# The last feed-forward stage of a hybrid trunk: the activations' sums moved ahead on VectorE, a weight sum by DMA, two subtractions moved

## The chip, the cores and the metric

The kernel runs on one core of a Trainium2 chip, in one launch. The metric is the device time in microseconds, the median of several executions. Below, PE is TensorE, DVE is VectorE, ACT is ScalarE, POOL is GpSimd and SP is SyncE; a name with a small q (SPq, POOLq, ACTq) is the queue of that engine, where it issues DMAs and waits on semaphores.

## The reference

A trunk of two layers on x (1, 512, 1024) in float32, each layer a token mixer and a SwiGLU feed-forward block (FFN), each with a norm before and behind it, and with shift, scale and gate from a conditioning vector. The part around the change is the last FFN:

```python
D_FF = 2816
def swiglu_ffn(h, w_in, w_out):
    gate, up = jnp.split(h @ w_in, 2, axis=-1)
    return (jax.nn.silu(gate) * up) @ w_out

h = rmsnorm(x, norm_g[i, 2]) * (1.0 + scale) + shift
y = swiglu_ffn(h, f_w_in[i], f_w_out[i])
x = x + gate * rmsnorm(y, norm_g[i, 3])
```

## The kernel before, in words

Every matrix product is taken with operands split into a high and a low part (`fp32r`): high x high, high x low and low x high, so three matmuls for one. A split is a cast on ACT (the high part) and a subtraction on DVE (the low part). Weights are loaded by DMAs from SP's queue into staging buffers (`wst`, two of them), split into `whl` (four buffers), and used by PE.

In the last FFN the order of the instructions on every engine is the order of the lines in the code. Both products of this stage are done with seven multiplications of half-size blocks instead of eight, as in Strassen's method, so sums and differences of activations and of weights are formed first.

*The lead and the whole chunks.* The hidden size 2816 is 22 column tiles of 128 for gate and 22 for up. Before the stage, six accumulations (`lead_ps[0..5]`, in the trace `li`) are begun for gate 0, gate 1, up 0, up 1, gate 2 and gate 3; `rest(i)` issues the second half of one of them. Two whole chunks follow (`more`, in the trace `ip`), for up 2 and up 3. `gate(f, pst)` (ACT) takes the silu, `up(f, pst)` (DVE, L1603) multiplies and writes `raw[:, f]`.

*The activations' sums.* `value(j)` (L1804) adds the high and low part of `h[j]` back together, into `va` (for j < 4, in a staging buffer of tag `wst`) or `vb`. `t_one` to `t_four` form differences of the token halves and split them into `tq`, the moving operands of P5, P6, P7 and P4. `t_low` is one split: the cast (L1807) and the subtraction (L1809, L1811).

*The unit loop.* Sixteen units u of 256 columns (two tiles) follow, alternately gate and up. `fetch(u)` issues the loads of a unit on SP's queue (L1626, L1627 into `sg`; L1629, L1630, L1632 into a staging buffer, `wsu`) and two accumulating DMAs on POOL's queue. `fetch(u + 2)` is issued as unit u begins. Each unit is seven products of 12 matmuls: P1, (P7 of the unit before), P5, P2, (P4 of the unit before), P6, P3. `split_x`, `split_y`, `split_z` and `split_s` make their weights, from sums by `sum_y` (L1666) and `sum_s` (L1670). `keep` copies a bank out on ACT (L1697), `c11`, `c12`, `c22` (L1713) and `c21` finish the four quarters of the output, and c21 of an up unit multiplies by the gate (L1721).

*The sums for the second product.* `s13` (L1593, L1594) forms two differences of quarters of `raw`, as soon as four tiles of `raw` are complete. `raw_done` calls it, from `up` or from c21.

*The second product.* Its weights lie in nine units (two of two row pairs, seven of one; a row pair p is 256 rows), in quarters `b11`, `b12`, `b21`, `b22`, loaded by `w2_load`. 77 steps, seven for each of 11 row pairs, are done two to a tile: 39 tiles n, each of 12 matmuls of 512 columns. Seven groups of steps follow one another: A (b11, a11), B (b21, a12), C (b22, a12), A (b22, a11), D (b12, s1), A (b11, a21), A (b21, a22); the trace calls their banks cA, cB, cC, cD. `w_prep(n + 4)` and `a_prep(n + 3)` prepare later tiles behind the matmuls of tile n (ACT L1743 and L1756, DVE L1744 and L1757). In between the weight quarters are changed in place: t1 (b12 += b11), t2 (b22 += b12) and t4 (b21 += b22) by accumulating DMAs on POOL's queue (L1619, SBUF to SBUF), t3 (b11 = b22 - b11) by a tensor operation on POOL (L1790). `behind(n)` says after which tile each is issued; t3 of row pair p stands behind tile 14 + p, t4 of unit i behind tile 14 + i.

Of the kernel before, what the change touches and what calls it, by code (L numbers as in the profile page):

```python
# [17 lines left out]
T = 512  # L18
# [17 lines left out]
def trunk_kernel(  # L36
# [533 lines left out]
    with ExitStack() as ph:  # L570
# [398 lines left out]
        def gate(f, pst):  # L969
            gates[f] = t2("g")  # L970
            act.activation(gates[f], pst, AF.Silu)

        def up(f, pst):
            g, a = gates[f], act_tile(f"ff{f}")
            dve.tensor_mul(g, pst, g)
            act.copy(a[:, 0, :], g)
            acts.append(a)
            lows.append(lambda: dve.tensor_tensor(a[:, 1, :], g, a[:, 0, :].bitcast(F32), SUB))
# [563 lines left out]
    with ExitStack() as ph:  # L1542
# [4 lines left out]
        NP = NF // 2  # L1547
# [28 lines left out]
        def b_(i, name, q=None):  # L1576

            t = rows_of[i][int(name[1]) - 1][:, :, slice(0, T) if name[2] == "1" else slice(T, D)]
            return t if q is None else t[:, q, :]

        def a_(name, p, n=1):
            if name == "s1":
                return s1t[:, p:p + n, :]
            c = int(name[2]) - 1
            v = raw[:, 2 * p:2 * (p + n), :].rearrange("p (i c) t -> p i c t", c=2)
            return v[:, :, c, slice(0, 256) if name[1] == "1" else slice(256, T)]
# [2 lines left out]
            gates[f] = t2("g")  # L1589
            act.activation(gates[f], pst, AF.Silu)  # L1590

        def s13(p, n):
            dve.tensor_tensor(a_("s1", p, n), a_("a21", p, n), a_("a22", p, n), SUB)  # L1593
            dve.tensor_tensor(a_("a21", p, n), a_("a11", p, n), a_("a21", p, n), SUB)  # L1594

        def raw_done(f):
            if f % 4 == 3:
                s13(f // 2 - 1, 2)
            elif f == NF - 1:
                s13(f // 2, 1)  # L1600

        def up(f, pst):
            dve.tensor_mul(raw[:, f, :], pst, gates[f])  # L1603
# [177 lines left out]
        with tc.manual_schedule(engines={PE_ENGINE, mybir.EngineType.SP, mybir.EngineType.Activation,  # L1781
# [2 lines left out]
            def t1(i):  # L1784
                add_(b_(i, "b12"), b_(i, "b11"))

            def t3(p):
                i = unit_of[p]
                q = units[i].index(p)
                pool.tensor_tensor(b_(i, "b11", q), b_(i, "b22", q), b_(i, "b11", q), SUB)  # L1790

            def t2_(i):
                add_(b_(i, "b22"), b_(i, "b12"))
# [9 lines left out]
                dst = va[:, j, :] if j < 4 else vb[j // 2 - 2][:, j % 2, :]  # L1803
                dve.tensor_add(dst, h[j][:, 0, :].bitcast(F32), h[j][:, 1, :].bitcast(F32))  # L1804

            def t_low(dst, src, sign=1.0):
                act.activation(dst[0], src, AF.Copy, scale=sign)  # L1807
                if sign == 1.0:
                    dve.tensor_tensor(dst[1], src, dst[0].bitcast(F32), SUB)  # L1809
                else:  # L1810
                    dve.scalar_tensor_tensor(dst[1], src, sign, dst[0].bitcast(F32), MUL, SUB)  # L1811

            def tq_of(i, ks):
                return [tq[i // 2][:, i % 2, hl, ks, :] for hl in range(2)]

            def t_one():
                dve.tensor_tensor(va[:, :, LO], va[:, :, LO], va[:, :, HI], SUB)
                t_low(tq_of(0, slice(0, 4)), va[:, :, LO])

            def t_two(b):  # L1820
                k = slice(2 * b, 2 * b + 2)
                dve.tensor_tensor(va[:, k, HI], vb[b][:, :, HI], va[:, k, HI], SUB)
                dve.tensor_add(vb[b][:, :, HI], vb[b][:, :, HI], va[:, k, LO])
                t_low(tq_of(1, k), vb[b][:, :, HI], -1.0)

            def t_three():
                t_low(tq_of(2, slice(0, 4)), va[:, :, HI])

            def t_four(b):
                k = slice(2 * b, 2 * b + 2)  # L1830
                dve.tensor_tensor(vb[b][:, :, LO], vb[b][:, :, HI], vb[b][:, :, LO], SUB)
                t_low(tq_of(3, k), vb[b][:, :, LO])

            for i, f in ((0, 0), (2, 0), (1, 1), (3, 1), (4, 2), (5, 3)):
                rest(i)
                if i in (2, 3):
                    up(f, lead_ps[i])
                else:
                    gate(f, lead_ps[i])
                if i == 1:  # L1840
                    for j in range(4):
                        value(j)
                elif i == 3:
                    t_one()
                elif i == 4:
                    for j in range(4, 8):
                        value(j)
            acc = in_chunk(more[0], h)
            split_x(0)
            for b in range(2):  # L1850
                t_two(b)
            sum_y(0)
            split_y(0)
            t_three()
            fetch(1)
            acc2 = in_chunk(more[1], h)
            sum_s(0)
            up(2, acc)
            split_s(0)
            for u in range(UN):  # L1860
                v = u - 1
                last = u == UN - 1
                if u + 2 <= UN:
                    fetch(u + 2)
                elif last:
                    tail = []
                    n12 = load_w([(w1, 21 * P, P), (w1, DFF + 20 * P, P)], later=tail)
                product(u, "P1")
                if u:
                    c12(v)  # L1870
                else:
                    up(3, acc2)
                    for b in range(2):
                        t_four(b)
                split_x(u + 1)
                if u:
                    product(v, "P7")
                keep(u, "A", 0, LO)
                product(u, "P5")
                if u:  # L1880
                    c22(v)
                product(u, "P2")
                keep(u, "C", 1, HI)
                if u:
                    product(v, "P4")
                c11(u)
                split_z(u)
                if not last:
                    sum_y(u + 1)
                    sum_s(u + 1)  # L1890
                product(u, "P6")
                if u:
                    c21(v)
                if last:
                    for op in tail[0]:
                        op()
                    n3 = load_w([(w1, DFF + 21 * P, P)], later=tail)
                else:
                    split_y(u + 1)
                product(u, "P3")  # L1900
                keep(u, "A", 0, HI)
                if not last:
                    split_s(u + 1)
# [24 lines left out]
            a_prep(0)  # L1928
            w_prep(0)
            tiles.append(in_chunk(n3[0], h))  # L1930
            up(20, tiles[2])
            w2_tile(4)
            w2_load(4, "b11")
# [1 line left out]
            a_prep(1)  # L1935
            w_prep(1)
            up(21, tiles[3])

            ht = [hp.tile([P, 1, D], F32, tag=f"h{j}", name=f"w2h{j}") for j in range(KD)]
            for i in range(5, len(units)):  # L1940
# [42 lines left out]
            def behind(n):  # L1983

                for i, u in enumerate(units):
                    if n - 8 == u[-1] // 2:
                        t2_(i)
                if 14 <= n < 14 + NP:
                    t3(n - 14)
                    if n - 14 < len(units):  # L1990
                        t4(n - 14)
                for t in range(2):
                    if n == 5:
                        got["11", t] = t2("c11")
                        act.copy(got["11", t], bank["A"][t])
                    elif n == 10:
                        dve.tensor_add(got["11", t], got["11", t], bank["B"][t])
                    elif n == 16:
                        got["12", t] = t2("c12")
                        act.copy(got["12", t], bank["C"][t])  # L2000
                    elif n == 21:
                        dve.tensor_tensor(got["12", t], got["12", t], bank["A"][t], SUB)
                    elif n == 27:
                        dve.tensor_add(got["12", t], got["12", t], bank["D"][t])
                        got["22", t] = spare[f"c22_{t}"]
                        act.copy(got["22", t], bank["D"][t])
                    elif n in (29, 30):
                        if t == n - 29:
                            square(t, 0, got["11", t])
                            square(t, 1, got["12", t])  # L2010
                    elif n == 32:
                        dve.tensor_tensor(got["22", t], got["22", t], bank["A"][t], SUB)  # L2012
                    elif n == 34:
                        square(2 + t, 0, got["22", t])
                        mean(t)
                        mean(2 + t)
                    elif n == 35:
                        root(t)
                        gated(got["22", t], 1, got["22", t])
                if n == 35:  # L2020
                    for t in range(2):
                        for hf, c in enumerate(("11", "12")):
                            x_new(t, hf, gated(got[c, t], hf, got[c, t]))
# [54 lines left out]
```

## Time and profile before

| | us |
|---|---|
| median of 3 runs | 1380.83 (1379.48 to 1382.18) |
| the profiled execution | 1380.38 |
| its span | 1378.3 |
| PE busy | 1337.6 (97%) |
| DVE busy | 998.5 (72%) |
| ACT busy | 618.6 (45%) |
| POOL busy | 80.0 (6%) |

A row of a timeline gives the start in microseconds from the span's start, the duration, the engine and the line, the operation, what it writes and reads, how many follow one another, and in brackets how long the engine stood idle before it and who released it. A row of waits gives who waited for whom, the total, the number of waits and the longest. Matmuls are pipelined, so the distance of their starts says more than the duration of one. In a row of windows, after the busy time of each engine, stand the granted PE clock (1.00 is full speed), the DMA engines' busy share and GB/s.

### The profile page before, as it was taken

How to read it: one execution, taken by the hardware profiler on the slowest of the kernel's cores; microseconds unless marked ns; L12 is line 12 of the kernel's file. 1: busy time of each engine (PE TensorE's matmuls, PEld its weight loads, DVE VectorE, ACT ScalarE, POOL GpSimd, SP SyncE). 2: the span in 40 equal slices, each digit the busy share in tenths (PEclk: the TensorE clock that was granted, in tenths of full speed). 3: DMA queues.
4: the chain of work that ended last, by engine and by line, in shares of the span. 5: the costliest groups of instructions: out<-in, count | busy, mean ns of one | idle time of the engine just before them, and what ended most of it. 6: DMA issues, size and time to landing. Idle time of an engine off the chain costs nothing.

```text
span 1378.3 us, 19120 instructions
## 1 busy us (share of the span) xinstructions
PE 1337.6 (97%) x7485; PEld 1151.1 (84%) x7485; DVE 998.5 (72%) x1570; ACT 618.6 (45%) x995; POOL 80.0 (6%) x93
## 2 busy tenths in 40 slices
PE   8999999999999999999999999999996999999976
PEld 6788889888888888898888888888896999998755
DVE  5588766777876323768988888886748677758886
ACT  5333355232222212745555554564743555545544
POOL 0000000000000000000000000000000121101530
PEclk9999999999999999999999999999997999999988
DMA  9767751777775323334534434233413887779731
GB/s 310 228 189 240 240 174 31 244 229 240 236 249 176 123 92 96 92 97 122 138 108 137 126 119 123 76 99 101 156 29 92 214 210 191 191 201 296 130 60 62
DMA packets 199886, 215.90 MB, mean 157 GB/s; under 512 B 8292, under 2 KB 148468, under 8 KB 198772
## 3 DMA queue, kind: packets, MB, share of 16 engines
q1 hardware_dynamic: 186384, 184.74, 43.3%
q0 software_dynamic: 9264, 17.04, 7.2%
q10 hardware_dynamic: 4148, 12.90, 2.9%
q8 instruction: 59, 0.97, 0.3%
q14 instruction: 31, 0.25, 0.1%
HBM read 195.37 MB, written 2.24 MB: 143 GB/s over the span
## 4 chain that ended last, share of the span: by engine, by line
PE 82%; DVE 6%; DMA 4%; issue 3%; SPq 2%; ACT 2%; POOL 1%; DVEq 0%; POOLq 0%; ACTq 0%
PE ip L276 14%; PE ip L278 14%; PE ip L277 14%; PE y L378 6%; PE y L379 6%; PE y L380 6%; PE sA L1687 4%; PE li L276 3%; PE li L278 3%; PE li L277 3%; DMA wsu<-in_f_w_in_dram 2%; PE sC L1687 2%; PE li L756 1%; DVE whlo L1744 1%; PE yd L1283 1%
## 5 line engine op out<-in xcount | busy, mean ns | idle before, releaser
L276 PE MATMUL ip<-h,whl 128*128 128x512 f32 x840 | 331.3, 394 | 0.2 <-DVE cv L863 0.2
L278 PE MATMUL ip<-h,whl 128*128 128x512 f32 x840 | 327.2, 390 | 0.0
L277 PE MATMUL ip<-h,whl 128*128 128x512 f32 x840 | 327.0, 389 | 0.0
L276 PEld LDWEIGHTS ip<-h,whl 128*128 128x128 f32 x840 | 157.8, 188 | 33.7 <-issue 1.8
L278 PEld LDWEIGHTS ip<-h,whl 128*128 128x128 f32 x840 | 157.7, 188 | 33.3
L277 PEld LDWEIGHTS ip<-h,whl 128*128 128x128 f32 x840 | 157.8, 188 | 31.7
L222 DVE TENSOR_TENSOR whl<-wst,whl 128x1024 fp32r<-128x1024 f32 x99 | 120.4, 1221 | 60.1 <-ACT whl L221 60.0
L124 DVE SCALAR_TENSOR_TENSOR ada_acc<-ada_st,csil,ada_acc 128x512 f32<-128x512 f32 x140 | 105.1, 750 | 3.5
L204 DVE TENSOR_TENSOR whlo<-wsto,whlo 128x1024 fp32r<-128x1024 f32 x41 | 49.9, 1224 | 78.5 <-ACT whlo L203 78.4
L221 ACT CAST whl<-wst 128x1024 fp32r<-128x1024 f32 x99 | 103.0, 1041 | 4.5 <-DMA wst<-in_m_w_in_dram 2.6
L1687 PE MATMUL sA<-tq,whl 128*128 128x256 f32 x576 | 76.1, 287 | 7.6 <-ACT g L1697 4.6
L276 PE MATMUL li<-h,whl 128*128 128x256 f32 x288 | 83.2, 289 | 0.0
L278 PE MATMUL li<-h,whl 128*128 128x256 f32 x288 | 81.5, 283 | 0.0
L277 PE MATMUL li<-h,whl 128*128 128x256 f32 x288 | 81.5, 283 | 0.0
L1687 PEld LDWEIGHTS sA<-tq,whl 128*128 128x128 f32 x576 | 72.7, 195 | 8.7 <-ACT g L1697 4.9
L203 ACT CAST whlo<-wsto 128x1024 fp32r<-128x1024 f32 x41 | 42.6, 1049 | 76.6 <-PE y L380 75.2
L378 PE MATMUL y<-whlo,ff 128*128 128x512 f32 x176 | 68.6, 390 | 0.0
L380 PE MATMUL y<-whlo,ff 128*128 128x512 f32 x176 | 68.5, 389 | 0.0
L379 PE MATMUL y<-whlo,ff 128*128 128x512 f32 x176 | 68.5, 389 | 0.0
L1142 DVE SCALAR_TENSOR_TENSOR cu<-ip,cols,cu 128x511 f32<-128x511 f32 (+2 forms) x84 | 62.8, 747 | 3.9 <-ACT cu L1139 1.4
L1778 PE MATMUL cA<-whlo,ao 128*128 128x512 f32 x264 | 61.4, 390 | 1.0 <-DVE w2h L2012 0.8
L1299 POOL TENSOR_TENSOR accg<-accg,sqg 128x512 f32<-128x512 f32 x7 | 9.1, 1297 | 879.3 <-ACT sqg L1297 879.3
(328 smaller groups left out, 2526.9 us busy)
## 6 DMA issues: line engine op xcount, KB each, us to landing
ada_st<-in_ada_w_dram SPq DMA_DIRECT2D x96, 512.0 KB, 5.2
wst<-in_f_w_in_dram SPq DMA_DIRECT2D x26, 1024.0 KB, 6.7
wst<-in_m_w_in_dram SPq DMA_DIRECT2D x14, 1024.0 KB, 5.4
wsto<-in_f_w_out_dram SPq DMA_DIRECT2D x10, 1024.0 KB, 5.1
wst<-in_m_w_in_dram SPq DMA_DIRECT2D x20, 512.0 KB, 5.3
wst<-in_a_w_in_dram SPq DMA_DIRECT2D x9, 1024.0 KB, 5.9
wsu<-in_f_w_in_dram SPq DMA_DIRECT2D x17, 512.0 KB, 5.6
csb<-cs_d ACTq DMA_DIRECT2D x8, 1024.0 KB, 5.4
```

Source lines behind the costliest of these rows:

```text
L124: dve.scalar_tensor_tensor(acc, w, csil[:, k:k + 1], acc, MUL, ADD)
L221: later.append((lambda sw=sw, w=w: act.copy(w[:, 0, :nk, :], sw), lambda sw=sw, w=w: dve.tensor_tensor(w[:, 1, :nk, :], sw, w[:, 0, :nk, : ...
L222: lambda sw=sw, w=w: dve.tensor_tensor(w[:, 1, :nk, :], sw, w[:, 0, :nk, :].bitcast(F32), SUB)))
L276: pe.matmul(dst, w_at(w, 0, kk), a[:, 0, sl], start=start, stop=False)
L277: pe.matmul(dst, w_at(w, 0, kk), a[:, 1, sl], start=False, stop=False)
L278: pe.matmul(dst, w_at(w, 1, kk), a[:, 0, sl], start=False, stop=stop)
L378: pe.matmul(pst, a[:, 0, tk], wt[:, 0, kk, :], start=k == 0, stop=False)
L379: pe.matmul(pst, a[:, 0, tk], wt[:, 1, kk, :], start=False, stop=False)
L380: pe.matmul(pst, a[:, 1, tk], wt[:, 0, kk, :], start=False, stop=k == K - 1)
L1142: dve.scalar_tensor_tensor(u[:, sft:], pst[:, :T - sft], w[3 - sft], u[:, sft:], MUL, ADD)
L1687: pe.matmul(dst, w[:, wl, k0 + k, :], moving(q, k, al), skip_group_check=True, start=q in ("P1", "P5", "P2") and k == 0 and i == 0, stop=k ...
L1778: pe.matmul(bank[r][sub], a[:, al, q, tk], w[:, hl, q, :], start=first and k == 0, stop=last and k == 2, skip_group_check=True)
```

## The change

Three edits, all in the last FFN. (a) The sums of the activations come first in DVE's order as the stage begins: `value` and `t_one` to `t_three` now stand ahead of the first `up`, the splits of unit 0 ahead of or between the `up` calls, `t_four` behind `up(2)` and behind P1 of unit 0; `fetch(1)` stands behind the last use of `va`, ahead of `rest(4)`. (b) `s13` is put into a list, and one of its two subtractions is issued behind c22 of each unit (the last ones behind two of the last chunks). (c) t3 isn't a tensor operation of POOL any more: b12 is loaded again from HBM into b11 by a plain DMA on ACT's queue behind tile 13 + i, and b22 is added from HBM by an accumulating DMA on POOL's queue behind tile 15 + i; t4 of unit i moves from tile 14 + i to tile 18 + i. The order of PE's matmuls is the same; ACT issues 11 more instructions (the loads), POOL's 11 tensor operations become 11 DMA issues.

```diff
-        def s13(p, n):
-            dve.tensor_tensor(a_("s1", p, n), a_("a21", p, n), a_("a22", p, n), SUB)
-            dve.tensor_tensor(a_("a21", p, n), a_("a11", p, n), a_("a21", p, n), SUB)
+        pending = []
 
         def raw_done(f):
             if f % 4 == 3:
-                s13(f // 2 - 1, 2)
+                p, n = f // 2 - 1, 2
             elif f == NF - 1:
-                s13(f // 2, 1)
+                p, n = f // 2, 1
+            else:
+                return
+            pending.append(lambda: dve.tensor_tensor(a_("s1", p, n), a_("a21", p, n), a_("a22", p, n), SUB))
+            pending.append(lambda: dve.tensor_tensor(a_("a21", p, n), a_("a11", p, n), a_("a21", p, n), SUB))
+
+        def s13(n=1):
+            for op in pending[:n]:
+                op()
+            del pending[:n]
...
-            def t3(p):
-                i = unit_of[p]
-                q = units[i].index(p)
-                pool.tensor_tensor(b_(i, "b11", q), b_(i, "b22", q), b_(i, "b11", q), SUB)
+            def t3_load(i):
+                for q, p in enumerate(units[i]):
+                    dma_s(b_(i, "b11", q), w2_rows(p)[:, 0, 0, T:])
+
+            def t3(i):
+                for q, p in enumerate(units[i]):
+                    add_(b_(i, "b11", q), w2_rows(p)[:, 0, 1, T:])
...
-            for i, f in ((0, 0), (2, 0), (1, 1), (3, 1), (4, 2), (5, 3)):
-                rest(i)
-                if i in (2, 3):
-                    up(f, lead_ps[i])
-                else:
-                    gate(f, lead_ps[i])
-                if i == 1:
-                    for j in range(4):
-                        value(j)
-                elif i == 3:
-                    t_one()
-                elif i == 4:
-                    for j in range(4, 8):
-                        value(j)
+            rest(0)
+            gate(0, lead_ps[0])
+            for j in range(4):
+                value(j)
+            dve.tensor_tensor(va[:, :, LO], va[:, :, LO], va[:, :, HI], SUB)
+            t_hi(one, va[:, :, LO])
+            rest(2)
+            value(4)
+            value(5)
+            t_lo(one, va[:, :, LO])
+            rest(1)
+            value(6)
+            value(7)
+            for b, k in enumerate(half):
+                dve.tensor_tensor(va[:, k, HI], vb[b][:, :, HI], va[:, k, HI], SUB)
+                dve.tensor_add(vb[b][:, :, HI], vb[b][:, :, HI], va[:, k, LO])
+                t_hi(tq_of(1, k), vb[b][:, :, HI], -1.0)
+            gate(1, lead_ps[1])
+            t_hi(three, va[:, :, HI])
+            rest(3)
+            for b, k in enumerate(half):
+                t_lo(tq_of(1, k), vb[b][:, :, HI], -1.0)
+            t_lo(three, va[:, :, HI])
+            fetch(1)
+            rest(4)
+            gate(2, lead_ps[4])
+            split_x(0)
+            sum_y(0)
+            rest(5)
+            gate(3, lead_ps[5])
             acc = in_chunk(more[0], h)
-            split_x(0)
-            for b in range(2):
-                t_two(b)
-            sum_y(0)
+            up(0, lead_ps[2])
             split_y(0)
-            t_three()
-            fetch(1)
+            up(1, lead_ps[3])
             acc2 = in_chunk(more[1], h)
             sum_s(0)
+            split_s(0)
             up(2, acc)
-            split_s(0)
+            t_four(0)
...
                 if u:
                     c12(v)
                 else:
+                    t_four(1)
                     up(3, acc2)
-                    for b in range(2):
-                        t_four(b)
...
                 if u:
                     c22(v)
+                    s13()
...
-                if 14 <= n < 14 + NP:
-                    t3(n - 14)
-                    if n - 14 < len(units):
-                        t4(n - 14)
+                    if n == 13 + i:
+                        t3_load(i)
+                    if n == 15 + i:
+                        t3(i)
+                    if n == 18 + i:
+                        t4(i)
```

`t_hi` and `t_lo` are the two halves of `t_low`, the cast and the subtraction; `one` and `three` are the tiles that `t_one` and `t_three` wrote.

More of the change, by code (lines that the diff above doesn't have):

```diff
@@ L1804, in value, with t_hi, t_lo @@
                 dve.tensor_add(dst, h[j][:, 0, :].bitcast(F32), h[j][:, 1, :].bitcast(F32))
-            def t_low(dst, src, sign=1.0):
+            def t_hi(dst, src, sign=1.0):
                 act.activation(dst[0], src, AF.Copy, scale=sign)
+            def t_lo(dst, src, sign=1.0):
                 if sign == 1.0:
@@ L1814, in tq_of, with t_four @@
                 return [tq[i // 2][:, i % 2, hl, ks, :] for hl in range(2)]
[L1816 to L1821, printed above, removed]
+            one, three = tq_of(0, slice(0, 4)), tq_of(2, slice(0, 4))
+            half = [slice(2 * b, 2 * b + 2) for b in range(2)]
+            def t_four(b):
+                k = half[b]
+                dve.tensor_tensor(vb[b][:, :, LO], vb[b][:, :, HI], vb[b][:, :, LO], SUB)
+                t_hi(tq_of(3, k), vb[b][:, :, LO])
+                t_lo(tq_of(3, k), vb[b][:, :, LO])
@@ L1823, in t_two @@
                 dve.tensor_add(vb[b][:, :, HI], vb[b][:, :, HI], va[:, k, LO])
[L1824 to L1832, printed above, removed]
-            for i, f in ((0, 0), (2, 0), (1, 1), (3, 1), (4, 2), (5, 3)):
-                rest(i)
-                if i in (2, 3):
-                    up(f, lead_ps[i])
-                else:
-                    gate(f, lead_ps[i])
-                if i == 1:
-                    for j in range(4):
-                        value(j)
-                elif i == 3:
-                    t_one()
-                elif i == 4:
-                    for j in range(4, 8):
-                        value(j)
+                t_hi(tq_of(1, k), vb[b][:, :, HI], -1.0)
@@ L1930, in trunk_kernel @@
             tiles.append(in_chunk(n3[0], h))
+            s13(2)
             up(20, tiles[2])
@@ L1937, in trunk_kernel @@
             up(21, tiles[3])
+            s13(2)
             ht = [hp.tile([P, 1, D], F32, tag=f"h{j}", name=f"w2h{j}") for j in range(KD)]
```

## The prediction

> **What bounds the kernel now.** I read the page first, then the waits of TensorE (PE) over the last feed-forward stage, then its timeline around each long wait, and then the timelines of the engines that the waits name. PE is busy 97% of the span, so time can only come from where PE stands still or runs at a low clock. From the page:
>
> ```profile
> span 1378.3 us, 19120 instructions
> ```
>
> The waits of PE from 1015 us to the end (total, times, longest):
>
> ```profile
> PE cD L1778 <- DVE ao L1757: 9.3, 2, 5.9
> PE sC L1687 <- ACT whl L1642: 5.7, 1, 5.7
> PE sA L1687 <- ACT g L1697: 4.6, 1, 4.6
> PE sA L1687 <- DVE g L1713: 3.1, 3, 1.0
> PE cC L1778 <- ACT ao L1756: 1.1, 1, 1.1
> ```
>
> Three groups: the start of the unit loop (sC, sA after ACT), three single microseconds inside the loop (sA after VectorE's g), and the second product's D part (cD). The change touches each of the three.
>
> **Part A, the sums first.** PE's timeline from the last two whole chunks (ip) on:
>
> ```profile
> 1032.12 0.40 PE L276 MATMUL ip<-h,whl 128*128 128x512 f32 x1
> ...
> 1042.80 0.39 PE L278 MATMUL ip<-h,whl 128*128 128x512 f32 x1
> 1043.02 1.60 PE L1687 MATMUL sA<-h,whl 128*128 128x256 f32 x12
> 1050.28 0.80 PE L1687 MATMUL sC<-tq,whl 128*128 128x256 f32 x2 [5.66 <-ACT whl L1642]
> ...
> 1061.16 2.93 PE L1687 MATMUL sA<-tq,whl 128*128 128x256 f32 x12 [4.56 <-ACT g L1697]
> ```
>
> and, from the chain of work, the same products once the clock is back:
>
> ```profile
> 1069.90 1.44 PE sC L1687 x12
> 1071.34 1.44 PE sB L1687 x12
> ```
>
> P1 of unit 0 starts at 1043.02, P5 of unit 1 at 1069.90. Between them lie seven products (P1, P5, P2, P6, P3 of unit 0, P1 of unit 1, P7 of unit 0), 7 x 1.44 = 10.1 us of matmul; they took 26.9. So 16.8 us are lost, 10.7 as waits and the rest in matmuls at a lower clock. VectorE (DVE) shows why:
>
> ```profile
> 1017.46 2.36 DVE L204 TENSOR_TENSOR whl<-wst,whl 128x1024 fp32r<-128x1024 f32 x2 [0.52 <-ACT whl L203]
> 1032.39 0.69 DVE L1603 TENSOR_TENSOR raw<-li,g 128x512 f32<-128x512 f32 x1 [12.57 <-PE li L278]
> 1032.99 2.49 DVE L1804 TENSOR_TENSOR va<-h 128x512 f32<-128x512 f32 x4
> ```
>
> The first `up` writes `raw`, and waits 12.57 us for the last lead matmul. In VectorE's order all eight `value` sums, the differences and the splits into `tq` stand behind it, though they need only `h`, which is ready. In the changed order `value` begins at 1019.8. By these rows 512 elements take 2.49 / 4 = 0.62 us and 1024 take 2.36 / 2 = 1.18. To the end of `t_lo(three)` there are 14 instructions of 512 and 3 of 1024: 14 x 0.62 + 3 x 1.18 = 12.2 us, and I add 1 us for handovers with ACT: done near 1033, just as PE leaves the lead. Then come split_x(0), sum_y(0), two `up`, split_y(0), sum_s(0) and split_s(0), 2 x 1.18 + 5 x 0.62 = 5.5 us, to 1039 or 1040. PE asks for split_x at 1043.0 and split_y at 1044.5, so both are early. The second wait (4.56 us) was for the copy of bank A, which stands behind split_x(1) on ACT; that needs the fetch of unit 1, whose loads were held up on the SP queue:
>
> ```profile
> SPq L1629 <- DVE tq L1809: 55.5, 1, 55.5
> ```
>
> ```profile
> 1052.64 0.37 SPq L1629 DMA_DIRECT2D wsu<-in_f_w_in_dram  x1
> ```
>
> These loads reuse the buffer of `va`, which `t_lo(three)` now frees 19 us earlier (near 1033 instead of 1052.6), so they have landed before ACT reaches the split near 1044; the copy is due at 1047.4. SP and POOL pass no other fetch, their order is the same. I book all 16.8 us. Next late would be `t_four(1)` and the last `up`, now near 1045, due in the next unit.
>
> **Part B, two subtractions moved.** Every fourth unit DVE runs them between c21 and split_y:
>
> ```profile
> 1114.12 3.14 PE L1687 MATMUL sA<-tq,whl 128*128 128x256 f32 x24 [1.02 <-DVE g L1713]
> 1155.72 3.14 PE L1687 MATMUL sA<-tq,whl 128*128 128x256 f32 x24 [1.02 <-DVE g L1713]
> ```
>
> Start to start is 41.60 us for four units of 7 x 1.44 = 10.08, so 1.28 us is lost each time, three times: 3.8 us. In the new place, one each in two units and behind c22, DVE comes next to a wait for bank B:
>
> ```profile
> 1166.17 0.42 DVE L1700 TENSOR_TENSOR g<-sB,g 128x256 f32<-128x256 f32 x1 [1.46 <-PE sB L1687]
> ...
> 1176.25 0.42 DVE L1700 TENSOR_TENSOR raw<-sB,raw 128x256 f32<-128x256 f32 x1 [0.59 <-PE sB L1687]
> ```
>
> One subtraction occupies 0.62 us and so fits into 1.46, and all but fits into 0.59. Without that cover it would cost 0.6 us in each of eight units. I book 3.8 us.
>
> **Part C, the third weight sum by DMA.** Eleven tensor operations leave POOL. DVE and POOL beside each other:
>
> ```profile
> L1744 DVE TENSOR_TENSOR whlo<-w2h,whlo 128x512 fp32r<-128x512 f32 x8 | 5.2, 688 | 1.4 <-ACT whlo L1743 1.4
> ```
>
> ```profile
> 1312.53 7.26 DVE L1744 TENSOR_TENSOR whlo<-w2t,whlo 128x512 fp32r<-128x512 f32 x1
> 1317.98 4.57 POOL L1790 TENSOR_TENSOR w2h<-w2h,w2h 128x512 f32<-128x512 f32 x2
> ```
>
> The first row (1260 to 1293 us, before POOL's tensor operations) has this form at 688 ns; beside POOL's one instruction takes 7.26 us. PE waits for DVE in just this stretch. All matmuls of the D part:
>
> ```profile
> L1778 PE MATMUL cD<-whlo,ao x66: 388/389/795, 1308.6 to 1337.2; 128*128 128x512 f32 x66
> ```
>
> The ip rows above give 10.68 us for 47 starts, 0.227 each; 65 starts are 14.8 us, and here 28.6 passed. Lost: 13.8 us (9.3 of waits, the rest at a low clock). The Trainium skill, page "SBUF — State Buffer", section "Who interferes with whom", says that a VectorE instruction with two SBUF inputs and a GpSimd instruction that reads SBUF lock each other out; the rows above agree. The same section warns that DMAs issued from GpSimd can starve while VectorE holds the shared pair; by that rule the new DMAs would crawl or stretch DVE as before. The trace speaks against it for this instruction: POOL issued such DMAs inside the 688 ns stretch. I book 13.8 us.
>
> What C adds: 11 plain loads of 256 KB on ACT's queue and 11 accumulating ones from HBM on POOL's. An issue on ACT takes 0.33 us by the nearest row, two per tile of 2.72 us (12 x 0.227) at most, and ACT stands idle for 1.04 per tile:
>
> ```profile
> L1129 ACTq DMA_DIRECT2D csb<-cs_d x8: 326/330/358, 615.7 to 857.5; - x8
> 1300.19 1.05 ACT L1743 CAST whlo<-w2t 128x1024 fp32r<-128x1024 f32 x1 [1.04 <-PE cA L1778]
> ```
>
> So the issues are hidden. The DMA engines are not idle there, though; the software queue from 1285 to 1300 us, and the hardware queue at full load from 1250 to 1260:
>
> ```profile
> q0 software_dynamic: 1191, 2.18, 85.7%
> ```
>
> ```profile
> 1250.00:1260.00 10.00, 10.00 (x46) 8.28 (x45) 9.89 (x18) 6.10 (x11) 2.13 (x2) 1.00 1.01 362
> 1293.51 0.86 POOL L1619 DMA_DIRECT2D w2h<-w2h  x1 [1.09 <-DVE ao L1757]
> 1294.76 1.26 ACT L1743 CAST whlo<-w2h 128x512 fp32r<-128x512 f32 x2
> ```
>
> 2.18 MB in 12.9 busy us is 1.5 us for 256 KB accumulated; a plain 256 KB at 362 GB/s is 0.7 us. Five or six loads are issued between 1288 and 1295, while the last sums of t2 are still moving; ACT reads those from 1294.76 on, with nothing to spare. They come some 4 us later (six loads of 0.7). ACT, waiting for them, also holds back `a_prep` of the tile that PE wants two tiles (5.4 us) later; casts and subtractions take some 2 of these, so about 3 us are covered. I estimate 1.5 us of stall and 0.5 of clock; the bounds are 0 (the loads slip in between) and 8 us (11 x 0.7, all on PE's path). Behind that there is room: a t3 sum is wanted ten tiles after its load is issued for unit 0 and seven for unit 8, so at least 19 us later, and t4 later still. The 11 + 11 accumulations of t3 and t4 fill 33 us of engine time, and do not outrun PE's use of them.
>
> **The sum.** 16.8 + 3.8 + 13.8 - 2 = 32.4 us. The profiled execution took 1380.38 us, 2.1 more than its span, and the median is 1380.83; from the median I get 1348.4.
>
> **The rivals.**
> (1) *The DMA queues collide.* The loads push t2, t3 and t4 back, and PE waits up to 8 us instead of 2: 1349 to 1355. For it: the 85.7% above. Against it: the landing times have slack after the first tiles. The Trainium skill, "DMA: Bandwidth & Descriptors", section "SWDGE vs HWDGE vs iDMA", has an engine take turns between hardware and software queues, which would halve the accumulations' rate while loads run; no run here shows it yet.
> (2) *The start is won only in part.* If the fetch of unit 1 lands after ACT reaches split_x(1), the 4.56 us wait and some 3 us of slow clock stay: 1356. The landing would have to take 10 us from 1033.
> (3) *DVE is stretched by POOL's issues too*, so C brings nothing: 1380.8 - 20.6 = 1360, or 1362 with the 2 us.
> (4) *Slower than before.* POOL's accumulations from HBM run one behind another, each waiting for its landing, as they might if POOL waits for the plain load each time. The last t3 is the 17th of 20 issues from 1293.5 on, and PE wants it ten tiles after the first D matmul, at 1308.6 + 27.2 = 1336. Spaced by s, PE waits 1293.5 + 17 s + 2.3 - 1336 (2.3 for its split): this eats the whole gain of 34 us from s = 4.4 us on; at 5.2, the landing time of such a DMA, it is 48 us, so 1395.
>
> ```profile
> w2h<-w2h POOLq DMA_DIRECT2D x4, 256.0 KB, 5.2
> ```
>
> Against it: in the same 15 us seven such DMAs were issued, so they overlap.
>
> **How the numbers follow.** The forecast has 0.70 (its own range 1345, if the 1.1 us of cC goes too and C costs nothing, to 1352), rival 1 beyond that 0.13, rival 2 0.07, rival 3 0.05, rival 4 0.03; 0.02 is left for a gain above 36 us. The range 1344 to 1357 takes in the forecast, rival 1 and rival 2, about 0.9, which I cut to 8 in 10 for steps that I have not seen. About 0.2% is what a measurement of this kernel can tell from no change. Faster by over 0.2%: all but rival 4 and a cancellation, 0.96; within: 0.01; slower: 0.03.
>
> **What would show it.** Right: no DVE instruction above 1.3 us in the second product; P1 of unit 0 to P5 of unit 1 in 10 to 11 us; no wait of PE inside the unit loop; the 66 D matmuls within 15 to 17 us; a small new wait of PE in the fourth of the seven products (cA). Wrong: PE waiting for t3 or t4 sums (a DMA landing named before ACT's whlo), a remaining wait at the copy of bank A, or DVE instructions still at 2 us and more while POOL issues. A time above 1362 would mean that the accumulations from HBM are the new bound.

## The result, and the profile after

The change makes the kernel faster, by less than forecast: 1359.86 us median (1359.40 to 1360.56, four runs) against 1381.07 us for the kernel before, a ratio of 0.9848 (95% interval 0.9831 to 0.9865). Forecast were 1348.4, in a range of 1344 to 1357; the time lies above that range. The profiled execution took 1359.75 us; its page begins:

```profile
span 1358.0 us, 19153 instructions
```

All three groups of waits are gone but for 0.3 us, and another has come. The waits of PE from 1000 us to the end, kernel after:

```profile
PE cA L1785 <- ACT ao L1763: 4.1, 2, 2.9
PE cA L1785 <- DVE w2h L2032: 2.7, 1, 2.7
PE cC L1785 <- ACT ao L1763: 1.4, 1, 1.4
PE cA L1785 <- DVE ao L1764: 0.4, 1, 0.4
PE sA L1694 <- DVE g L1720: 0.3, 1, 0.3
```

Of the waits at sC and sA 0.3 us is left, and cD is not in the list at all. New are the three rows at cA, four waits of 7.2 us together (0.8 us of the one after `DVE w2h` stood there before, too). PE's timeline shows where the gain was made and where part of it was given back:

```profile
1042.92 1.60 PE L1694 MATMUL sA<-h,whl 128*128 128x256 f32 x12
...
1052.99 1.60 PE L1694 MATMUL sC<-tq,whl 128*128 128x256 f32 x12
1056.31 3.14 PE L1694 MATMUL sA<-tq,whl 128*128 128x256 f32 x24 [0.28 <-DVE g L1720]
...
1305.87 6.28 PE L1785 MATMUL cA<-whlo,ao 128*128 128x512 f32 x27
1315.01 5.49 PE L1785 MATMUL cA<-whlo,ao 128*128 128x512 f32 x12 [2.86 <-ACT ao L1763]
1321.72 3.83 PE L1785 MATMUL cA<-whlo,ao 128*128 128x512 f32 x14 [1.22 <-ACT ao L1763]
1325.90 2.60 PE L1785 MATMUL cA<-whlo,ao 128*128 128x512 f32 x10 [0.36 <-DVE ao L1764]
1331.23 16.84 PE L1785 MATMUL cA<-whlo,ao 128*128 128x512 f32 x66 [2.73 <-DVE w2h L2032]
```

The seven products at the start take 10.07 us instead of 26.88. The A part on b11, which follows the D part and reads the sums of t3, takes from 1305.87 to 1331.23, 25.4 us for 63 matmuls that take 14.3 us at the undisturbed pace (0.227 us each).

Placed side by side, by the first and last start of each bank's matmuls:

| | before | after | gained so far |
|---|---|---|---|
| cA starts (second product begins) | 1246.6 | 1226.6 | 20.0 |
| cC | 1276.5 to 1293.7 | 1256.5 to 1275.6 | 18.1 at its end |
| cD | 1308.6 to 1337.2 | 1290.2 to 1305.6 | 31.6 at its end |
| last cA | 1367.6 | 1347.7 | 19.9 |

The D part gives 13.2 us, and the two A parts behind it lose 11.7. Who is late there is to be seen on ACT, which casts the b11 quarters (timeline of ACT, after):

```profile
1306.91 0.62 ACT L1750 CAST whlo<-w2s 128x512 fp32r<-128x512 f32 x1 [2.26 <-DMA w2s<-in_f_w_out_dram]
...
1313.82 0.62 ACT L1750 CAST whlo<-w2h 128x512 fp32r<-128x512 f32 x1 [2.25 <-DMA w2h<-in_f_w_out_dram]
1314.34 0.61 ACT L1763 CAST ao<-raw 128x512 fp32r<-128x512 f32 x1
1316.90 0.62 ACT L1750 CAST whlo<-w2h 128x512 fp32r<-128x512 f32 x1 [1.95 <-DMA w2h<-in_f_w_out_dram]
1320.53 0.62 ACT L1750 CAST whlo<-w2h 128x512 fp32r<-128x512 f32 x1 [3.01 <-DMA w2h<-in_f_w_out_dram]
```

ACT waits for the landing of t3's accumulations (they are the ones that read `in_f_w_out_dram`), and the cast `ao<-raw` for PE stands behind each wait in ACT's order. So PE's row names ACT, ACT's row names the DMA, and POOL's timeline tells why the DMA was late:

```profile
1280.06 0.86 POOL L1626 DMA_DIRECT2D w2t<-in_f_w_out_dram  x1 [3.38 <-issue]
...
1288.43 0.86 POOL L1626 DMA_DIRECT2D w2t<-in_f_w_out_dram  x1 [2.22 <-issue]
1292.97 1.22 POOL L1626 DMA_DIRECT2D w2t<-w2t  x1 [3.68 <-issue]
1294.64 0.92 POOL L1626 DMA_DIRECT2D w2s<-in_f_w_out_dram  x1 [0.45 <-issue]
1299.31 1.21 POOL L1626 DMA_DIRECT2D w2t<-w2t  x1 [3.75 <-issue]
...
1315.40 0.87 POOL L1626 DMA_DIRECT2D w2h<-in_f_w_out_dram  x1 [0.41 <-issue]
```

The rows `w2t<-w2t` are t4's, beginning with t4(0); those whose issue takes 1.2 us carry 512 KB. Between the first t3 at 1280.06 and the last at 1315.40 stand 18 transfers of 256 KB, ten of t3 and eight of t4, so 1.96 us each. The DMA queues from 1280 to 1322 us (packets, MB, share of 16 engines) keep the engines busy for 97% of the time:

```profile
q0 software_dynamic: 3054, 5.63, 82.5%
q10 hardware_dynamic: 731, 1.33, 9.6%
q1 hardware_dynamic: 288, 0.52, 4.8%
```

### The profile page after: what moved, and what is told of

Read it like the earlier page. It is cut to its first block, busy times and chain, and to the rows that moved or that the text cites. A ratio compares the mean times of both kernels' runs of the same rounds, so it can differ in the third digit from the quotient of the medians.

```text
span 1358.0 us, 19153 instructions
## 1 busy us (share of the span) xinstructions
PE 1334.3 (98%) x7485; PEld 1147.6 (85%) x7485; DVE 979.6 (72%) x1570; ACT 618.2 (46%) x995; POOL 74.8 (6%) x93
## 4 chain that ended last, share of the span: by engine, by line
PE 88%; issue 4%; POOL 2%; DMA 2%; SPq 2%; DVE 1%; ACT 1%; POOLq 0%; DVEq 0%; ACTq 0%
PE ip L276 14%; PE ip L278 14%; PE ip L277 14%; PE sA L1694 6%; PE y L378 6%; PE y L379 6%; PE y L380 6%; PE sC L1694 3%; PE li L276 3%; PE li L278 3%; PE li L277 3%; PE sB L1694 2%; PE li L756 1%; PE yd L1283 1%; PE yo L1277 1%
## 5 line engine op out<-in xcount | busy, mean ns | idle before, releaser
L1785 PE MATMUL cA<-whlo,ao 128*128 128x512 f32 x264 | 66.5, 410 | 7.2 <-ACT ao L1763 4.1
L1785 PEld LDWEIGHTS cA<-whlo,ao 128*128 128x128 f32 x264 | 51.8, 198 | 21.0 <-ACT ao L1763 8.4
```

The lines of the kernel that those rows point to most:

```text
L1785: pe.matmul(bank[r][sub], a[:, al, q, tk], w[:, hl, q, :], start=first and k == 0, stop=last and k == 2, skip_group_check=True)
```

## The experiments

The theory: A, B and the D part brought what was forecast, and the loss is t3's sums arriving late, because on POOL's queue, which issues in order, they take turns with t4's, at 1.96 us for each 256 KB. The rivals: the loss comes from the total of the transfers, whatever their order; from VectorE, as before; or from the start of the stage.

### e1_sums_subs, e2_t3_vector, e3_t3_out: parts A and B, with three ways to make t3

All three are the changed kernel with t3 and t4 at their old places. e1 has t3 as POOL's tensor operation as before, e2 puts the same operation on VectorE, e3 has none:

```diff
-                    if n == 13 + i:
-                        t3_load(i)
-                    if n == 15 + i:
-                        t3(i)
-                    if n == 18 + i:
-                        t4(i)
+                if 14 <= n < 14 + NP:
+                    t3(n - 14)           # e1: pool.tensor_tensor, e2: dve.tensor_tensor
+                    if n - 14 < len(units):
+                        t4(n - 14)
```

> Parts A and B alone: the sums first on DVE and the two subtractions moved, t3 as a tensor operation on POOL as before. Theory (A and B brought 16.8 and 3.3 us, part C nothing on balance): the trace of the changed kernel reaches the first matmul of the second product 20.0 us earlier than before, so 1381.1 - 20 = 1361, and the 66 D matmuls take 28 us again. Rival (A and B brought less, and C some of its 13.8): 1365 or more.

Measured: 1362.13 us (1360.63 to 1363.75), ratio 0.9859 (0.9844 to 0.9874).

> A and B, and t3 as a tensor operation on DVE instead of POOL, at the old place (t4 too). No DMA is added and nothing runs on POOL beside DVE. Theory (the DMAs of t3 cost what the end of the contention gave): D within 16 us, no wait in the A part behind it, 1361 - 13.8 = 1347, up to 2 us more where DVE is full. Rival (the A part would wait anyway, for t2 and t4 or for ACT): 1357 to 1360.

Measured: 1347.35 us (1346.29 to 1348.71), ratio 0.9752 (0.9738 to 0.9767).

> A and B, t3 left out: b11 keeps the old weights, so the sixth group of products works on other numbers; t4 at its old place. It bounds what any placing of t3 can bring. Theory: 1346 to 1347. Rival (waits of the A part have another cause): 1357 to 1360.

Measured: 1346.19 us (two runs), ratio 0.9743 (0.9724 to 0.9763).

So A and B alone take 19.5 us off 1381.6, and t3 on DMAs adds only 2.3 to that where t3 on VectorE adds 14.8, within some 1 us of having no t3. In e1 the old loss stands where it stood; waits of PE from 1200 us on and VectorE's timeline in the D part:

```profile
PE cD L1785 <- DVE ao L1764: 8.5, 2, 5.0
```

```profile
1288.44 4.51 DVE L1764 TENSOR_TENSOR ao<-s1t,ao 128x512 fp32r<-128x512 f32 x1
1292.87 7.25 DVE L1751 TENSOR_TENSOR whlo<-w2t,whlo 128x512 fp32r<-128x512 f32 x1
```

The same operation in e2, as a group from 1270 to 1325 us with the splits beside it:

```profile
L1764 DVE TENSOR_TENSOR ao<-s1t,ao 128x512 fp32r<-128x512 f32 x5 | 3.4, 682 | 0.0
L1797 DVE TENSOR_TENSOR w2t<-w2t 128x512 f32<-128x512 f32 x5 | 3.4, 684 | 0.0
```

Eleven operations of 0.68 us on VectorE are 7.5 us of its own time, and VectorE has most of that to spare here: PE waits 2.3 us in the C part (1.4 in e1 and e3) and 0.8 at the last cA, as in e1 and e3, and nowhere else in the second product.

### e4_t4_behind and e10_t4_ahead: the order on POOL's queue

The same transfers and bytes as the changed kernel, in another order: in e4 all of t3 leaves ahead of t4, in e10 all of t4 ahead of the last t3.

```diff
-                    if n == 18 + i:
+                    if n == 24 + i:       # e4
                         t4(i)
```

```diff
-                    if n == 15 + i:
+                    if n == 18 + i:       # e10
                         t3(i)
-                    if n == 18 + i:
+                    if n == 14 + i:
                         t4(i)
```

> The changed kernel with t4 of unit i issued behind tile 24 + i instead of 18 + i, so all t3 go ahead of all t4 on POOL's in-order queue. If the order on that queue is what made t3 late (six t4 stand ahead of the last t3, some 8 x 1.6 us): the last t3 lands near 1308 instead of 1320, PE's 4.5 us of waits before cA and the slow clock go, 1349 to 1353. If the DMA engines' time as a whole is the bound (they are 96% busy from 1280 to 1320), t4 is late instead and waits move to the last group: 1356 to 1361.

Measured: 1349.07 us (1348.25 to 1350.20), ratio 0.9767 (0.9751 to 0.9783).

> The changed kernel with the order on POOL's queue turned the other way: t4 of unit i behind tile 14 + i, t3 behind 18 + i, so all t4 stand ahead of the last t3 (11 transfers of 256 KB ahead of it instead of 8; e4 has none). Theory (t3 late by its place in the queue, at 1.96 us for 256 KB, as the trace of the changed kernel has it): the last t3 is issued near 1280 + 21 x 1.96 = 1321 instead of 1315.4, PE waits some 6 us longer, 1364 to 1367. Rival (the place hardly matters, total traffic does): 1359 to 1361.

Measured: 1365.19 us (two runs, 1364.63 and 1365.76), ratio 0.9879 (0.9857 to 0.9901). The last t3 in e4 and in e10, and PE's longest wait of e10:

```profile
1301.38 0.88 POOL L1626 DMA_DIRECT2D w2h<-in_f_w_out_dram  x1 [0.50 <-issue]
```

```profile
1321.32 0.88 POOL L1626 DMA_DIRECT2D w2h<-in_f_w_out_dram  x1 [0.42 <-issue]
```

```profile
PE cD L1785 <- ACT ao L1763: 11.1, 1, 11.1
```

With 0, 8 and 11 transfers of t4 ahead of it, the last t3 leaves at 1301.38, 1315.40 and 1321.32, and the times are 1349.07, 1359.86 and 1365.19. From the changed kernel to e10 it is 5.9 us later and the time 5.3 us longer; from e4 to the changed kernel 14.0 us later and 10.8 us longer, the rest being slack. PE's long wait in e10 is for another sum, though: the fifth t3, of row pair 4, which the A part reads first. It leaves only at 1306.08, behind eight transfers of t4, and ACT, which stands still for it, holds back PE's operands for the end of the D part. Behind it the chain of work that ended last still goes through the last t3 and its landing. ACT's row and the chain's:

```profile
1311.01 0.62 ACT L1750 CAST whlo<-w2t 128x512 fp32r<-128x512 f32 x1 [14.67 <-DMA w2t<-in_f_w_out_dram]
```

```profile
1321.32 5.60 DMA w2h<-in_f_w_out_dram
1326.95 0.62 ACT whlo L1750
```

So e10's time came as expected, but not by a longer wait for the last sum alone. The order is the cause; with equal bytes, "too much traffic" would have left e4 at 1356 or more. In e4 PE goes through the A part from 1305.87 to 1321.44, 15.6 us where the changed kernel takes 25.4. Its clock stays up as well (windows of e4, then of the changed kernel):

```profile
1310.00:1320.00 10.00, 10.00 (x46) 8.21 (x44) 7.49 (x11) 8.89 (x18) 5.66 (x6) 1.00 0.80 137
```

```profile
1310.00:1320.00 10.00, 7.14 (x22) 5.17 (x20) 2.73 (x5) 3.03 (x6) 5.21 (x6) 0.71 1.02 166
```

The cA waits are 7.2 us in the changed kernel and 1.4 in e4, 5.8 between them; the other half of the loss is matmuls at a lower granted clock behind these waits (0.71 in the row above), as at the start of the stage before.

### e11_t4_halves: why the issues stand 2 us apart

```diff
-                add_(b_(i, "b21"), b_(i, "b22"))
+                for q in range(len(units[i])):
+                    add_(b_(i, "b21", q), b_(i, "b22", q))
```

> The changed kernel with t4 of the two double units issued as two accumulating DMAs of 256 KB each instead of one of 512 KB; bytes and order the same. What is told apart is why POOL's issues stand 3 to 4 us apart. If a 512 KB accumulation must find room for all its descriptors on the software queue before it starts, halves are issued earlier and the transfers behind them too: the last t3 leaves 2 to 3 us earlier than 1315.4, and the time is 1355 to 1358. If the DMA engines' time for the bytes sets the spacing, nothing moves: last t3 within 1 us of 1315.4, 1359 to 1361.

Measured: 1357.73 us (1357.43 to 1359.80), ratio 0.9828 (0.9812 to 0.9845). The last t3 and the software queue from 1280 to 1322 us:

```profile
1314.71 0.87 POOL L1626 DMA_DIRECT2D w2h<-in_f_w_out_dram  x1 [0.77 <-issue]
```

```profile
q0 software_dynamic: 3200, 5.82, 84.0%
```

The last t3 leaves 0.7 us earlier, and 18 transfers from 1280.51 on are 1.90 us each instead of 1.96: the mark that was set for the engines' time. The time speaks the other way: the median lies in the range of the first expectation, and only the profiled execution, the longest of the four at 1359.80, in that of the second. The interval overlaps that of the changed kernel, so the time by itself decides nothing, and what spaces the issues is not settled. The size of the queue's ring was not changed in any run.

### e5_load_only: the plain loads by themselves

```diff
-                    if n == 15 + i:
-                        t3(i)
```

> The changed kernel with t3's accumulating DMA left out: the plain load of b12 into b11 stays, b22 is not added to it. The software queue then carries t2 and t4 alone, the hardware queue the same 2.9 MB of loads. If the accumulations of t3 behind t4 are the whole loss, the time is 1346 to 1348.5, as without t3 at all (1346.19). If the plain loads have a price of their own (t2 pushed back at the start of the D part), it is 1349 to 1352.

Measured: 1349.06 us (1348.53 to 1349.29), ratio 0.9766 (0.9751 to 0.9780): at the lower edge of the second expectation. It is 2.9 us above e3. In the profiled executions 1.6 of it is a step of the clock in the C part, which e2 shows as well, without these loads (the last section). That doesn't leave 1.3 us as the price of the loads: e4, which has them and not that step, loses about as much to the late t2 sums (see "Why the prediction was wrong"), so the 2.9 can't be divided with these runs. Of the 13.7 us between e3 and the changed kernel, 10.8 go with the accumulating DMAs of t3.

### e7_t3_dma_alone, e8_sums_alone: one part alone, on the kernel before

e7 has only part C, e8 only part A, edited as in the diff of the change.

> Part C alone on the kernel before: t3 by a plain load and an accumulating DMA, t4 behind tile 18 + i. Theory (what D wins, the A part behind it loses): 66 D matmuls within 16 us instead of 28.6, PE waits before cA as in the changed kernel, 1379 to 1381.5, which is less than 0.2% from before. Rival (the collision comes only with the earlier start of parts A and B): 1368 to 1370.

Measured: 1379.73 us (1377.79 to 1380.75, ten runs), ratio 0.9984 (0.9975 to 0.9994).

> Part A alone: the sums first, both subtractions at their old place, t3 on POOL as before. Theory: 1381.6 - 16.8 = 1364.8, with PE's three waits of 1.0 us in the unit loop still there; against e1 it gives part B, 3 us. Rival (the moved subtractions are needed for the start too): above 1367.

Measured: 1365.61 us (1364.86 to 1367.40), ratio 0.9886 (0.9867 to 0.9904). Part A alone is worth 15.7 us, B on top of it 3.5 (e8 less e1), and part C alone 1.6. In e7 the D part is as short as it can be, all the same:

```profile
L1778 PE MATMUL cD<-whlo,ao x66: 389/389/389, 1311.7 to 1327.1; 128*128 128x512 f32 x66
```

That is 15.4 us instead of 28.6. But the A part behind it waits for t3, as in the changed kernel:

```profile
PE cA L1778 <- ACT ao L1756: 4.3, 2, 2.5
PE cA L1778 <- DVE w2h L2017: 1.9, 1, 1.9
```

### e9_t3_vector_16: the best version, two tiles later

```diff
-                if 14 <= n < 14 + NP:     # of e2
-                    t3(n - 14)
-                    if n - 14 < len(units):
-                        t4(n - 14)
+                if 16 <= n < 16 + NP:
+                    t3(n - 16)
+                if 14 <= n < 14 + len(units):
+                    t4(n - 14)
```

> e2 with t3 on DVE two tiles later (behind tile 16 + p), so that it stands clear of the wait for the t2 sums, where PE stood still for 2.3 us in e2 against 1.4 in the run without t3. Theory: 1.5 to 2 us less than e2, near 1346. Rival (DVE is simply full there, or the later t3 delays other splits): 1347 to 1349.

Measured: 1348.50 us (1346.53 to 1349.56), ratio 0.9756 (0.9740 to 0.9773). This was a miss: PE's wait in the C part shrank from 2.3 to 1.5 us, and the time didn't follow, since the slow matmuls behind that wait stayed. e2 remains the fastest complete version, 12.5 us under the change as made; e2 and e4 can't be told apart by these intervals.

## Why the prediction was wrong

**Part A, right.** 16.8 us booked, 16.8 seen at the start of the loop (26.88 less 10.07); e8's time gives 15.7, and its trace shows one wait of PE for VectorE's g more than before (0.49 us at 1056.80). The loads of unit 1 left SP's queue at 1033.1, as booked, and PE waited neither for the split nor for the copy of bank A. **Part B, right.** The start of the second product lies 20.0 us earlier, so 3.2 fall to it, and 3.5 by e8 and e1; booked were 3.8. The 0.28 us wait at 1056.31 is what remains, once.

**Part C, the gain.** 13.8 us booked in the D part, 13.2 seen; three matmuls of bank cA stand among the 66, so the undisturbed part takes 15.4 us and not the 14.8 of the prediction. No operation of VectorE in the second product takes over 1.3 us:

```profile
L1751 DVE TENSOR_TENSOR whlo<-w2h,whlo 128x512 fp32r<-128x512 f32 x28 | 18.8, 688 | 19.3 <-ACT whlo L1750 19.3
```

The rule of the Trainium skill ("SBUF — State Buffer", "Who interferes with whom") that DMAs issued from GpSimd can starve while VectorE holds the shared pair was set aside for these operations. The section itself says that a `tensor_tensor` was not seen to stall DMAs, which the prediction left out. The traces agree with that: POOL issued 20 such DMAs from 1280 us on, VectorE's operation of two SBUF inputs stayed at 688 ns, and the DMA engines were busy for 97% of that time, so they were not starved. What the same section says of two engines' tensor operations is what e1 and e2 show: 7.25 us beside POOL's subtraction, 0.68 without it. Rival 3 is out: that the time falls on its figure of 1360 is a coincidence.

**Part C, the cost: here the prediction failed.** The step is the sentence that the accumulations of t3 and t4 "do not outrun PE's use of them", with a price of 2 us for all of C, all of it for t2: the accumulations of t3 and t4 were put at nothing. Those of t3, coming late, cost 10.8 us (the changed kernel less e4, where they come ahead of t4, or less e5, which has none). The prediction's own sign of being wrong, a DMA landing named before ACT's `whlo`, is what ACT's rows show. Three things were wrong in it.

The price of one transfer. 1.5 us for 256 KB came from 2.18 MB in 12.9 *busy* us. By the wall the same row gives 2.18 MB in 15 us, or 1.80 us for each 256 KB (0.262 MB), and that is what the queue does when it is loaded and little runs beside it: in e3 t4's eleven go from 1276.90 to 1294.91, in ten steps of 1.80. With the loads and the other hardware queue beside it, it is 1.96.

The order. The slack of "at least 19 us" was reckoned for one transfer, from its own tile to its use. But t3 and t4 share a queue that issues in order, and t4 of unit i, wanted one part later, stands ahead of t3 of unit i + 3. The last t3 has 18 transfers ahead of it from the first on; at 1.96 these are 35.3 us.

The start. The first t3 was taken to leave as t3 did before, 1293.5 less the 20 us gained; it left 6.5 us after that, at 1280.06. The last sum of t2 had left only at 1275.82; for the 3.38 us idle in front of the first t3 the profile names no releaser, so that it waited for room behind t2 is argued and not shown. The late t2 itself, for which the 2 us were booked, cost PE no wait in this execution: ACT stood 4.0 us for it from 1255 to 1300, and PE has no wait between 1271 and 1312.

```profile
ACT whlo L1750 <- DMA w2h<-w2h: 4.0, 3, 2.5
```

But PE came to that place 1.5 us late, after the step of the clock in the C part (the last section). Where that step is missing, with the same loads, PE does pay for t2. The same stretch in the changed kernel, then in e4:

```profile
1275.80 14.59 PE L1785 MATMUL cA<-whlo,ao 128*128 128x512 f32 x63
1290.23 14.44 PE L1785 MATMUL cD<-whlo,ao 128*128 128x512 f32 x63
```

```profile
1274.28 6.28 PE L1785 MATMUL cA<-whlo,ao 128*128 128x512 f32 x27
1280.90 9.49 PE L1785 MATMUL cA<-whlo,ao 128*128 128x512 f32 x36 [0.34 <-ACT ao L1763]
1290.22 14.44 PE L1785 MATMUL cD<-whlo,ao 128*128 128x512 f32 x63
```

In e4 the 36 matmuls take 9.3 us from start to start in place of 8.2, and D begins at the same time; e10 and e11 are alike (D from 1290.07 and 1290.65). So the late t2 costs PE about 1.5 us there, near the 2 booked, and the 10.8 us come on top of it. Why the 36 matmuls are slower at a granted clock of 1.00 stays open.

By the chain of work that ended last, the last t3 lands 5.10 us after its issue, and ACT's cast follows at once:

```profile
1315.40 5.10 DMA w2h<-in_f_w_out_dram
1320.53 0.62 ACT whlo L1750
```

That is 1320.5, and its split takes 2.3 more, 1322.8. PE would want it ten tiles after its first D matmul, 1290.2 + 27.2 = 1317.4, so it is 5.4 us late; PE waited 4.4 in that part and 2.7 behind it, and lost the rest of the 10.8 us in slow matmuls. This is the mechanism of rival 1, with 10.8 us in place of its 8 at most; its bound counted the loads and not the queue. Rival 4 had the right quantity, the issue time of the last t3, but its formula has no landing time, starts at 1293.5, and was asked only where the gain would be gone (s = 4.4). With s = 1.96, the later start and the 5.1 us of landing it turns from a margin of 7 us into a wait of some 5 (an estimate).

In e4, t3's eleven leave between 1279.99 and 1301.38 with the plain loads beside them, 2.14 us each, and t4's between 1304.69 and 1321.95 without, 1.73. The rule of the Trainium skill ("DMA: Bandwidth & Descriptors", "SWDGE vs HWDGE vs iDMA"), that an engine takes turns between hardware and software queues, fits in that both share the engines; the accumulations' rate fell by a fifth, and was not halved. The loads didn't run all that time, however: from 1280 to 1303 us the two hardware queues took 25% of the engines' time (1.85 MB of 4.58). What the rate is while loads run without a break, these runs don't show.

## What to carry to other kernels

For work on an in-order queue, reckon the issue time of the last item that is wanted, from the queue's first one and with everything that stands in between, by bytes over wall time from a stretch in which that queue was loaded; the distance from an item's own place to its use says nothing on this. Where two streams share such a queue, put the one that is wanted first wholly ahead: that alone was 10.8 us here. And before work leaves one engine for DMAs, try it on the other engine that has room: eleven subtractions of 0.68 us on VectorE were 12.5 us better than the transfers.

## What was not expected of the hardware

- A stall of PE of the same length cost one of two amounts. The wait in the C part is 1.4 to 1.8 us in ten of the profiled executions. Behind it 15 matmuls take 5.64 or 5.65 us in four (the changed kernel after 1.45, e5 after 1.74, e7 after 1.70, e9 after 1.51), with a granted clock of 0.91 over the 20 us around it, and 4.05 to 4.09 us at 1.00 in six (e1 after 1.42, e3 1.37, e4 1.38, e8 1.80, e10 1.65, e11 1.64). So 1.6 us come or don't; what decides it was not found. It need not show in the time: e4, e10 and e11, without the step, reach the D part at about the same time as the changed kernel, behind the late t2 sums.
- Accumulating DMAs of 256 KB keep a steady 1.73 to 1.80 us (146 to 152 GB/s of payload) with little beside them on the engines, and 1.9 to 2.1 beside plain loads. Half-size issues change it by 3% (1.96 to 1.90).
- Part C alone shortened the D part by 13.2 us and the kernel by 1.6: where the operands of the next part are late, a part that ends earlier leads to an earlier wait.
